# Expert stage of a two-block transformer kernel: order of the score blocks, place of their weight loads, depth of the row gathers

## The chip, the cores and the metric

One Trainium2 chip, one core of it. The metric is the device time of one execution in microseconds (us); less is better. The kernel before takes 3052.63 us, the median of 3 runs (3047.12 to 3056.36).

## The reference, cut to what matters

Two transformer blocks run on 512 tokens of width 1024 in float32. The change lies in the second half of the first block, `peer_ffn`: a mixture of 16384 experts, each of which is one row of a table `u` and one row of a table `v`.

```python
q = (xb @ wq).reshape(T, HEADS, 2, 128)
s = einsum('thpc,hpnc->thpn', q, keys)           # scores against 2 x 128 keys per head
v1, i1 = top_k(s[:, :, 0], 16); v2, i2 = top_k(s[:, :, 1], 16)
sc, pos = top_k(all sums v1 + v2, 16)            # 16 experts per head, 8 heads
idx = i1 * 128 + i2 at pos; gate = softmax(sc)
act = gelu(einsum('td,thkd->thk', xb, u_tab[idx]))
out = einsum('thk,thkd->td', gate * act, v_tab[idx])
```

So every token has 128 of the 16384 experts, and what it needs is gelu(x . u) of each, times its gate, times that expert's row of v, summed.

## The kernel before, in words

**Two ways for two groups of tokens.** Tokens 0 to 383 (`ND`) are computed densely: for all 16384 experts, in 128 blocks of 128, the kernel computes gelu(u_block . x) for every token, multiplies it with a gate table that is zero where the token did not choose the expert, and adds the product with the block's rows of v into six PSUM banks. Tokens 384 to 511 are computed sparsely: their 256 rows (128 of u, 128 of v) are gathered one at a time, row s of all 128 tokens in one indirect DMA from GpSimd (POOL), 512 KB each, into a tile `row`.

**Score blocks.** `s_block(b)` (lines 721 to 739) takes the weights of block b from `uld`, fetches those of block b + 1 if they are not fetched (`u_load`, 713 to 719: one 512 KB DMA on SP's queue into one of three buffers, a rounded copy `uh` on ScalarE (ACT), the rest `ul` on VectorE (DVE), both in three buffers), issues 24 matmuls into one of two PSUM buffers, and evicts them on ACT with Gelu into `st`. Blocks 0 to 13 (`LEAD`) stay on chip in `held`; blocks 14 to 71 (up to `NS`) go to DRAM by a 192 KB DMA on SP (line 737), from one of two buffers, and come back later (`s_again`, 741); blocks 72 to 127 are computed inside the last loop.

**Order in time.** First the queries and the top 16 keys of every head (lines 798 to 819, the matmuls against `keys` on line 812). Then `route(3)`, which gives `idx` of the sparse tokens, `route(0)`, and `gates(0)`, `gates(1)`, `gates(2)`, one for each 128 dense tokens. `gates` (905 to 929) makes the gate table in steps of 8 tokens (`q`): two one-hot tiles `o` on DVE (913), scaling on ACT (916), 16 matmuls into `pg` (920), two evictions into `stg` (921), and for every 32 tokens a 2 MB store of `stg` to `gates_d` on SP (927). In each step `fill(1)` adds one score block and `row_u()` one gathered row of u: it issues the gather of row n + 2 and multiplies row n with the token on DVE (756). In `gates(2)` every second step takes two rows. Rows of this part have three buffers, and there are 56 (`U1`) of them. `fill` ends at block 64 (`NS - HOLD`), which is four steps before the end of `gates(2)`.

**Between the gates and the loop** stand the last seven score blocks, 65 to 71, on lines 1000 to 1017. From line 993 on (`manual_schedule`) each engine keeps the written order; ahead of it the framework orders the instructions of each engine itself. As written, SP's order there is: weights of 66, the first two blocks of v (`v_dma`, 957), weights of 67, store of 65, weights of 68, store of 66, and so on, with the first gate tile (`v_gate(0)`, a 768 KB read of `gates_d`) after the store of 67. On ACT the rounding of block b + 2's weights stands ahead of the Gelu of block b, and the store of block b waits for that Gelu.

**The loop** (1018 to 1044), b = 0 to 127: prepare block b + 1 (`g_mul` and the split of the gated scores, `v_hi` on ACT, `v_lo` on DVE), read scores back or compute a new block, use the gathered rows that are due (`gs`), then 18 matmuls of block b (1043). Up to b = 57 the scores are read back, afterwards a score block is computed in each step. Here rows have eight buffers.

Pools are stacked: those of the stage up to the gates (`hp4`, `tp4q`, `np4`, `tp4`, `rp4`) are closed before those of the loop (`vpool`, `gp`) open in the same memory, and a new tile waits for the readers of what lay there. `keys` (line 768) takes 8 KB of each partition in `hp4` and is read on line 812 alone.

Of the kernel before, what the change touches and what calls it, by code (L numbers as in the profile page):

```python
# [8 lines left out]
F32 = mybir.dt.float32  # L9
# [39 lines left out]
def tile_two_blocks(ctx: ExitStack, tc: tile.TileContext, a: dict, out: bass.AP):  # L49
# [3 lines left out]
    def mk(c, name, bufs, space=None, side=None):  # L53
        kw = dict(space=space) if space is not None else {}
        return c.enter_context(tc.tile_pool(name=name, bufs=bufs, side=side, reuse_waits="tile", **kw))
# [640 lines left out]
    def blin(w, kd, loeng=None):  # L696
        return Lin(wb, w, kd, loeng, bufs=3, rbufs=3)

    with ExitStack() as c1:
# [5 lines left out]
        gw = pk.tile([128, 128], F32, name="gw")  # L705
        act = pk.tile([128, 128], F32, name="act")
        coef = pk.tile([128, 128], F32, name="coef")
        G.memset(acc, 0.0)
        held = {}
        uld = {}  # L710
        rows = {}

        def u_load(b):
            raw = wb.tile([128, KD, 128], F32, tag="wraw", name="uraw", bufs=3)
            nc.sync.dma_start(raw, a["peer_ut"][b])
            uh = wb.tile([128, KD, 128], F32R, tag="whi", name="uh")
            ul = wb.tile([128, KD, 128], F32R, tag="wlo", name="ul")
            split_r(uh, ul, raw, V)
            uld[b] = (uh, ul)

        def s_block(b):
            if b not in uld:
                u_load(b)
            uh, ul = uld.pop(b)
            if b + 1 < 128 and b + 1 not in uld:
                u_load(b + 1)
            ps = pss.tile([128, ND], F32, tag="pss", name="pss")
            n = 0
            for w_, x_ in ((uh, lo), (ul, hi), (uh, hi)):
                for k in range(KD):  # L730
                    PE.matmul(ps, w_[:, k, :], x_[:, k, :ND], start=n == 0, stop=n == 23)  # L731
                    n += 1
            st = pk.tile([128, ND], F32, tag="st" if b < LEAD or b >= NS else "sp", name="st",
                         bufs=LEAD + 2 if b < LEAD or b >= NS else 2)
            S.activation(st, ps, AF.Gelu)  # L735
            if LEAD <= b < NS:
                nc.sync.dma_start(st_d[b - LEAD], st)
            else:
                held[b] = st
# [5 lines left out]
        def gather_dma(s, pool):  # L745
            if s >= 256:
                return
            tab, i = (a["peer_u"], s) if s < 128 else (a["peer_v"], s - 128)
            r = rows[s] = pool.tile([128, D], F32, tag="row", name="row", bufs=8 if s >= U1 else 3)
            G.indirect_dma_start(out=r, out_offset=None, in_=tab,  # L750
                                 in_offset=bass.IndirectOffsetOnAxis(ap=idx[:, i:i + 1], axis=0))

# [10 lines left out]
        with ExitStack() as c2:  # L763
# [1 line left out]
            pps = mk(c2, "pps4", 2, PSUM)  # L765
            ppt = mk(c2, "ppt4", 2, PSUM)
            ppg = mk(c2, "ppg4", 2, PSUM)
            keys = hp_.tile([128, 16, 128], F32, name="keys")
            nc.sync.dma_start(keys, a["keys"])
            io = hp_.tile([128, 128], F32, name="io")  # L770
            G.iota(io, pattern=[[1, 128]], base=0, channel_multiplier=0, allow_small_or_imprecise_dtypes=True)
            vals = hp_.tile([128, 4, 8, 2, 16], F32, name="vals")
# [10 lines left out]
            with ExitStack() as c3:  # L783
                tp = mk(c3, "tp4q", 2)
                np_ = mk(c3, "np4", 3)
                lin = blin(a["wq"], KD)
                for f in range(2):
                    lin.load(f)

                def normed(k):  # L790
                    h = np_.tile([128, T], F32, tag="h", name="h")
                    V.scalar_tensor_tensor(h, xt[:, k, :], vv("norm2_w", k), rb2, op0=ALU.mult, op1=ALU.mult)
                    split_r(hi[:, k, :], lo[:, k, :], h, G)
                    pt = ppt.tile([128, 512], F32, tag="pt", name="pt")
                    PE.transpose(pt[:, :128], h[:, ND:], ident)
                    S.activation(htok[:, k * 128:(k + 1) * 128], pt[:, :128], AF.Copy)

                first_ps = [pps.tile([128, 512], F32, tag="ps", name="ps") for n in range(2)]
                lin.mm_rows([(first_ps[f], f) for f in range(2)], hu, lu)
                for f in range(16):  # L800
                    if f < 2:
                        ps = first_ps[f]
                    else:
                        ps = pps.tile([128, 512], F32, tag="ps", name="ps")
                        lin.mm(ps, f, hu, lu)
                    if f + 2 < 16:
                        lin.load(f + 2)
                    q = tp.tile([128, T], F32, tag="q", name="q")
                    V.tensor_mul(q, ps, rb2)
                    ps = ppt.tile([128, 512], F32, tag="pt", name="ps")  # L810
                    for t in range(4):
                        PE.matmul(ps[:, t * 128:(t + 1) * 128], q[:, t * 128:(t + 1) * 128], keys[:, f, :],
                                  start=True, stop=True)
                    s_ = tp.tile([128, 4, 128], F32, tag="s", name="s", bufs=2)
                    S.activation(s_.rearrange("p t n -> p (t n)"), ps, AF.Copy)
                    for t in range(4):
                        top16(vals[:, t, f // 2, f % 2], ids[:, t, f // 2, f % 2], s_[:, t, :])
                    if f < KD:
                        normed(f)
# [70 lines left out]
            def fill(n):  # L890
                for _ in range(n):
                    if done_[0] < NS - HOLD:
                        s_block(done_[0])
                        done_[0] += 1

            def row_u():

                n = done_[1]
                if n < U1:
                    if n + 2 < U1:  # L900
                        gather_dma(n + 2, rp)
                    gather(n)
                    done_[1] += 1

            def gates(t, tr, other):

                for hf in range(128 // TS):
                    stg = tp.tile([128, 128, TS], F32, tag="stg", name="stg", bufs=2)
                    for q in range(TS // 8):
                        t0 = hf * TS + q * 8  # L910
                        oo = [tp.tile([128, 8, 128], F32, tag=f"o{n}", name=f"o{n}") for n in range(2)]
                        for n in (1, 0):
                            V.tensor_tensor(oo[n], io[:, None, :].to_broadcast([128, 8, 128]),  # L913
                                            tr[:, n, t0:t0 + 8, None].to_broadcast([128, 8, 128]), op=ALU.is_equal)
                        for i in range(8):
                            S.activation(oo[0][:, i, :], oo[0][:, i, :], AF.Copy, scale=tr[:, 2, t0 + i:t0 + i + 1])
                        for e in (0, 4):
                            pg = ppg.tile([128, 4, 128], F32, tag="pg", name="pg")
                            for i in range(4):
                                PE.matmul(pg[:, i, :], oo[1][:, e + i, :], oo[0][:, e + i, :], start=True, stop=True)  # L920
                            S.activation(stg[:, :, q * 8 + e:q * 8 + e + 4], pg.rearrange("p t i -> p i t"), AF.Copy)
                        fill(1)
                        row_u()
                        if t == NT_ - 1 and q % 2:
                            row_u()
                        next(other, None)
                    nc.sync.dma_start(gates_d[t * (128 // TS) + hf], stg)
                for _ in other:
                    pass
# [3 lines left out]
            for n, _ in enumerate(route(NT_, trs)):  # L933
                if n % 2:
                    fill(1)
            for s in range(2):
                gather_dma(s, rp)
            for n, _ in enumerate(route(0, trs)):
                fill(1)
# [9 lines left out]
        with ExitStack() as c2:  # L949
# [46 lines left out]
            def gs(b):  # L996
                return U1 + (256 - U1) * sum(cost[:b]) // sum(cost)


            for b in range(NS - HOLD, NS - HOLD + 2):  # L1000
                if b not in uld:
                    u_load(b)
            for b in range(2):
                v_dma(b, False)
            for b in range(NS - HOLD, NS - 2):
                u_load(b + 2)
                s_block(b)
                if b == NS - HOLD + 2:
                    v_gate(0)
            g_mul(0)  # L1010
            g_split(0)
            v_hi(0)
            v_lo(0)
            for s in range(gs(0), gs(1)):
                gather_dma(s, gp)
            for b in range(NS - 2, NS):
                s_block(b)
            for b in range(128):
                n = b + 1
                if b + 2 < 128:  # L1020
# [452 lines left out]
```

## Time and profile before

| | |
|---|---|
| median of 3 runs | 3052.63 us (3047.12 to 3056.36) |
| the profiled execution, its time | 3042.29 us |
| its span in the trace | 3040.5 us |
| TensorE (PE) busy in the span | 95% |
| DVE, ACT, POOL busy | 62%, 39%, 30% |
| granted TensorE clock, mean | 0.977 of 2.4 GHz |

Times of rows are us from the start of the span. PE is TensorE's matmuls, PEld its weight loads; SPq and POOLq are the queues from which DMAs are issued. Idle time stands in brackets ahead of an instruction, with what ended it. Matmuls are pipelined, so their durations overlap; a score block's 24 matmuls are best read by the distance from one block to the next.

### The profile page before, as it was taken

Reading aid. Unit: us, or ns where it says so; the run is one execution under the profiler, and the core shown is the slowest. Engines: PE = TensorE matmul, PEld = TensorE weight load, DVE = VectorE, ACT = ScalarE, POOL = GpSimd, SP = SyncE. Lnnn points to the kernel's source line nnn. Section 1 sums busy time; section 2 is a strip of 40 time slices with the busy share of each in tenths; the row PEclk is TensorE's granted clock in tenths of the full one; section 3 lists DMA queues with packets and bytes.
Section 4 is the critical chain, followed back from the end, with each engine's and each line's share of the span. In section 5 each row is a group of like instructions: output and inputs, shape, how many; then the busy total and the mean of one; then the engine's idle time right before and its main releaser. Section 6 shows DMA issues by size and latency. Waiting matters only on the chain.

```text
span 3040.5 us, 45240 instructions
## 1 busy us (share of the span) xinstructions
PE 2877.7 (95%) x17733; PEld 2402.8 (79%) x17733; DVE 1896.8 (62%) x3317; ACT 1198.8 (39%) x2073; POOL 924.9 (30%) x584
## 2 busy tenths in 40 slices
PE   8897898999989799999999999999999999999998
PEld 6676776799989677799999977888876666788886
DVE  7567638899987377777777786332258744643311
ACT  6344334237867233333333334332234343433322
POOL 1011135211321111133444324444431233244443
PEclk9899989999999899999999999999999999999999
DMA  3240123257876699999899962333321112323332
GB/s 115 63 129 27 41 77 122 70 164 257 315 271 241 239 303 318 311 327 306 307 315 332 313 218 63 97 97 95 99 93 49 56 56 66 101 91 97 97 96 78
DMA packets 201286, 494.92 MB, mean 163 GB/s; under 512 B 17328, under 2 KB 95152, under 8 KB 199152
## 3 DMA queue, kind: packets, MB, share of 16 engines
q1 hardware_dynamic: 164208, 357.78, 36.0%
q0 software_dynamic: 36864, 134.23, 12.7%
q8 instruction: 140, 2.29, 0.3%
q14 instruction: 74, 0.61, 0.1%
HBM read 446.60 MB, written 45.22 MB: 162 GB/s over the span
## 4 chain that ended last, share of the span: by engine, by line
PE 59%; DVE 21%; issue 7%; ACT 4%; DMA 4%; POOL 2%; SPq 0%; ACTq 0%; DVEq 0%; POOLq 0%
PE ps L141 33%; PE pss L731 8%; PE pv L1043 8%; DVE vl L978 2%; DVE row L756 2%; ACT vh L972 2%; DVE o L913 2%; PE ps L318 2%; DVE ul L71 2%; DMA gate<-gates_d 2%; DMA uraw<-peer_ut 1%; PE po L1287 1%; DVE st L983 1%; PE pg L920 1%; PE ps L1263 1%
## 5 line engine op out<-in xcount | busy, mean ns | idle before, releaser
L71 POOL TENSOR_TENSOR wlo<-wraw,whi 128x1024 fp32r<-128x1024 f32 (+4 forms) x232 | 503.6, 2174 | 775.9 <-ACT whi L70 773.7
L70 ACT ACTIVATE whi<-wraw 128x1024 fp32r<-128x1024 f32 (+4 forms) x320 | 261.7, 823 | 692.2 <-PE ps L141 428.6
L750 POOL DMA_INDIRECT row<-peer_u,idx x128 | 158.1, 1235 | 618.2 <-DVE row L756 427.6
L141 PE MATMUL ps<-lo,whi 128*128 128x512 f32 x1112 | 303.4, 402 | 2.3 <-DVE pad L218 1.4
L141 PE MATMUL ps<-hi,whi 128*128 128x512 f32 x1112 | 295.1, 395 | 0.0
L141 PE MATMUL ps<-hi,wlo 128*128 128x512 f32 x1112 | 293.9, 395 | 1.1 <-POOL wlo L71 0.7
L141 PEld LDWEIGHTS ps<-lo,whi 128*128 128x128 f32 x1112 | 208.1, 190 | 55.6 <-issue 11.0
L1043 PE MATMUL pv<-vl,gh 128*128 128x512 f32 x768 | 243.1, 398 | 6.8 <-DVE vl L978 4.3
L141 PEld LDWEIGHTS ps<-hi,wlo 128*128 128x128 f32 x1112 | 208.0, 189 | 51.5 <-issue 6.3
L750 POOL DMA_INDIRECT row<-peer_v,idx x128 | 168.6, 1317 | 256.7 <-DVE acc L761 219.3
L141 PEld LDWEIGHTS ps<-hi,whi 128*128 128x128 f32 x1112 | 207.6, 188 | 47.1 <-issue 5.2
L1043 PE MATMUL pv<-vh,gl 128*128 128x512 f32 x768 | 239.0, 392 | 1.9 <-ACT vh L972 1.9
L1043 PE MATMUL pv<-vh,gh 128*128 128x512 f32 x768 | 239.6, 393 | 0.0
L70 ACT ACTIVATE gh<-st 128x384 fp32r<-128x384 f32 x128 | 67.2, 525 | 414.2 <-DVE st L983 224.2
L731 PE MATMUL pss<-lo,uh 128*128 128x384 f32 x1024 | 210.5, 347 | 17.6 <-ACT st L735 17.4
L731 PE MATMUL pss<-hi,ul 128*128 128x384 f32 x1024 | 203.4, 339 | 4.0 <-DVE ul L71 4.0
L731 PEld LDWEIGHTS pss<-lo,uh 128*128 128x128 f32 x1024 | 183.2, 192 | 23.6 <-ACT st L735 19.2
L731 PE MATMUL pss<-hi,uh 128*128 128x384 f32 x1024 | 199.5, 336 | 0.0
L978 DVE TENSOR_TENSOR vl<-vraw,vh 128x1024 fp32r<-128x1024 f32 x128 | 161.4, 1261 | 50.1 <-ACT vh L972 49.7
L71 DVE TENSOR_TENSOR ul<-uraw,uh 128x1024 fp32r<-128x1024 f32 x128 | 156.2, 1220 | 53.3 <-ACT uh L70 53.3
L731 PEld LDWEIGHTS pss<-hi,ul 128*128 128x128 f32 x1024 | 182.6, 191 | 4.7 <-DVE ul L71 4.7
L1043 PEld LDWEIGHTS pv<-vl,gh 128*128 128x128 f32 x768 | 141.4, 189 | 52.0 <-DVE vl L978 23.6
(445 smaller groups left out, 5236.6 us busy)
## 6 DMA issues: line engine op xcount, KB each, us to landing
uraw<-peer_ut SPq DMA_DIRECT2D x128, 512.0 KB, 6.2
vraw<-peer_v SPq DMA_DIRECT2D x128, 512.0 KB, 5.5
wraw<-ffn_w_in SPq DMA_DIRECT2D x88, 512.0 KB, 3.5
gates_d<-stg SPq DMA_DIRECT2D x12, 2048.0 KB, 9.2
gate<-gates_d SPq DMA_DIRECT2D x32, 768.0 KB, 8.1
wraw<-w_in SPq DMA_DIRECT2D x40, 512.0 KB, 3.5
wraw<-ffn_w_out SPq DMA_DIRECT2D x32, 512.0 KB, 3.5
st_d<-st SPq DMA_DIRECT2D x58, 192.0 KB, 4.2
```

Of the source, the lines that this page charges most:

```text
L70: S.activation(hi, src, AF.Copy)
L71: eng.tensor_sub(lo, src, hi)
L141: PE.matmul(ps, w_[:, k, :m], x_[:, k0 + k, :], start=n == 0, stop=n == last)
L318: PE.matmul(ps[j:j + 64], w_[j:j + 64], x_[j:j + 64], start=start, stop=stop, tile_position=(j, j))
L731: PE.matmul(ps, w_[:, k, :], x_[:, k, :ND], start=n == 0, stop=n == 23)
L750: G.indirect_dma_start(out=r, out_offset=None, in_=tab, in_offset=bass.IndirectOffsetOnAxis(ap=idx[:, i:i + 1], axis=0))
L756: V.scalar_tensor_tensor(r, r, 1.0, htok, op0=ALU.mult, op1=ALU.mult, accum_out=act[:, s:s + 1])
L913: V.tensor_tensor(oo[n], io[:, None, :].to_broadcast([128, 8, 128]), tr[:, n, t0:t0 + 8, None].to_broadcast([128, 8, 128]), op=ALU.is_equal)
L920: PE.matmul(pg[:, i, :], oo[1][:, e + i, :], oo[0][:, e + i, :], start=True, stop=True)
L972: S.activation(vh, vld[b], AF.Copy)
L978: V.tensor_sub(vl, raw, vh)
L1043: PE.matmul(pv[t * 2 + e], l_[:, ts_], r_[:, e * 512:(e + 1) * 512], start=b == 0 and q == 0, stop=b == 127 and q == 2)
```

## The change

1. The score blocks are computed in another order, `seq`: blocks 14 to 71 first, then 0 to 13, then 72 to 127. So the seven blocks between the gates and the loop are 7 to 13, which stay on chip and are not stored. (The prediction counts blocks by their place in the order; places 65 to 71 are those between the gates and the loop, in both kernels.)
2. In the last four steps of `gates(2)` the weights of places 66 and 67 are fetched and rounded.
3. The part between the gates and the loop is written anew: one block of v (not two) is fetched after place 65, the gate tile and the second block of v after place 67; POOL copies one column of the scores of place 68 into a tile `fence`, and its gathers stand behind that copy; the preparation of loop step 0 stands after place 69.
4. Rows of u up to 56 have five buffers in place of three, and row n + 4 in place of n + 2 is gathered ahead; four rows in place of two are gathered before `route(0)`.
5. `keys` moves from the pool `hp4` to the pool `np4`, which is closed before the gates begin.

```diff
+        fence = pk.tile([128, 1], F32, name="fence")
+        seq = list(range(LEAD, NS)) + list(range(LEAD)) + list(range(NS, 128))
+        place = {b: n for n, b in enumerate(seq)}
...
-            if b + 1 < 128 and b + 1 not in uld:
-                u_load(b + 1)
+            n = place[b] + 1
+            if n < 128 and seq[n] not in uld:
+                u_load(seq[n])
...
-            r = rows[s] = pool.tile([128, D], F32, tag="row", name="row", bufs=8 if s >= U1 else 3)
+            r = rows[s] = pool.tile([128, D], F32, tag="row", name="row", bufs=8 if s >= U1 else 5)
...
-            keys = hp_.tile([128, 16, 128], F32, name="keys")
-            nc.sync.dma_start(keys, a["keys"])
...
+                keys = np_.tile([128, 16, 128], F32, name="keys", bufs=1)
+                nc.sync.dma_start(keys, a["keys"])
...
-                        s_block(done_[0])
+                        s_block(seq[done_[0]])
...
-                    if n + 2 < U1:
-                        gather_dma(n + 2, rp)
+                    if n + 4 < U1:
+                        gather_dma(n + 4, rp)
...
+                        if t == NT_ - 1 and hf == 128 // TS - 1 and q >= 2:
+                            for n in seq[done_[0]:done_[0] + q]:
+                                if n not in uld:
+                                    u_load(n)
...
-            for s in range(2):
+            for s in range(4):
                 gather_dma(s, rp)
...
-            for b in range(NS - HOLD, NS - HOLD + 2):
-                if b not in uld:
-                    u_load(b)
-            for b in range(2):
-                v_dma(b, False)
-            for b in range(NS - HOLD, NS - 2):
-                u_load(b + 2)
-                s_block(b)
-                if b == NS - HOLD + 2:
+            for n in range(NS - HOLD, NS):
+                if n < NS - 2 and seq[n + 2] not in uld:
+                    u_load(seq[n + 2])
+                s_block(seq[n])
+                if n == NS - HOLD:
+                    v_dma(0, False)
+                if n == NS - HOLD + 2:
                     v_gate(0)
-            g_mul(0)
-            g_split(0)
-            v_hi(0)
-            v_lo(0)
-            for s in range(gs(0), gs(1)):
-                gather_dma(s, gp)
-            for b in range(NS - 2, NS):
-                s_block(b)
+                    v_dma(1, False)
+                if n == NS - 4:
+                    G.tensor_copy(fence, held[seq[n]][:, 0:1])
+                    for s in range(gs(0), gs(1)):
+                        gather_dma(s, gp)
+                if n == NS - 3:
+                    g_mul(0)
+                    g_split(0)
+                    v_hi(0)
+                    v_lo(0)
```

## Rows read from the trace of the kernel before

**Rows 1.** Busy time in stretches of the expert stage (columns in the first row).

```profile
core 0: us, PE busy (x) PEld busy (x) DVE busy (x) ACT busy (x) POOL busy (x), PEclk, DMA share, GB/s
700.00:860.00 160.00, 158.73 (x1055) 158.45 (x1056) 157.85 (x247) 134.23 (x337) 31.62 (x23) 0.98 0.76 267
890.00:945.00 55.00, 46.68 (x292) 46.00 (x291) 42.09 (x54) 33.21 (x85) 19.35 (x14) 0.94 0.89 321
993.00:1043.00 50.00, 32.56 (x154) 31.18 (x154) 8.55 (x9) 9.62 (x14) 7.33 (x7) 0.83 0.66 233
```

**Rows 2.** The chain that ended last, 960 to 1046: start us, us, what.

```profile
960.18 4.17 PE pss L731 x24
964.35 1.78 PE pg L920 x16
...
995.54 10.74 DMA uraw<-peer_ut
...
1040.81 3.45 DMA uraw<-peer_ut
```

**Rows 3.** What PE waited for, 993 to 1045.

```profile
PE pss L731 <- ACT st L735: 17.4, 4, 9.5
```

**Rows 4.** What ACT waited for, 993 to 1045: us in total, times, longest.

```profile
ACT uh L70 <- DMA uraw<-peer_ut: 40.1, 6, 12.6
```

**Rows 5.** Order of time on SP's queue: the last store of the gate table.

```profile
993.75 0.32 SPq L927 DMA_DIRECT2D gates_d<-stg  x1
```

**Rows 6.** What PE waited for, 840 to 992.

```profile
PE pg L920 <- ACT stg L921: 9.0, 2, 4.5
PE pg L920 <- ACT o L916: 3.8, 1, 3.8
```

**Rows 7.** What DVE waited for, 840 to 992.

```profile
DVE row L756 <- DMA row<-peer_u,idx: 20.2, 10, 6.4
```

**Rows 8.** Stretches with a lower granted clock (columns as in rows 1).

```profile
883.00:887.00 4.00, 3.70 (x18) 3.70 (x19) 4.00 (x6) 1.97 (x4) 3.35 (x2) 0.57 0.82 258
...
900.00:907.00 7.00, 5.79 (x23) 5.80 (x24) 7.00 (x8) 6.25 (x18) 1.85 (x2) 0.52 1.02 390
...
1002.00:1013.00 11.00, 5.21 (x16) 5.21 (x17) 1.23 (x1) 1.43 (x2) 6.39 (x6) 0.53 1.01 390
...
1050.50:1054.00 3.50, 3.50 (x10) 2.73 (x9) 2.65 (x3) 1.38 (x2) 0.00 (x0) 0.51 0.99 340
```

**Rows 9.** Order of time on PE at the loop's start.

```profile
1042.41 0.63 PE L1043 MATMUL pv<-vh,gl 128*128 128x512 f32 x2
...
1048.62 0.73 PE L1043 MATMUL pv<-vh,gl 128*128 128x512 f32 x2 [1.93 <-ACT vh L972]
1049.88 0.50 PE L1043 MATMUL pv<-vl,gh 128*128 128x512 f32 x1 [0.52 <-DVE vl L978]
```

**Rows 10.** Issue to landing of gathered rows, 700 to 990.

```profile
DMA to landing us min/median/max: 4.2/7.6/13.0
```

**Rows 11.** Evictions of stored score blocks, 660 to 697: min/median/max ns, first to last.

```profile
L735 ACT ACTIVATE st<-pss x8: 491/493/495, 663.2 to 692.3; 128x384 f32<-128x384 f32 x8
```

**Rows 12.** Order of time on POOL, 984 to 1012: first and last of eight gathers.

```profile
988.51 0.99 POOL L750 DMA_INDIRECT row<-peer_u,idx  x1 [47.67 <-ACT o L916]
...
1009.73 0.94 POOL L750 DMA_INDIRECT row<-peer_u,idx  x1 [0.30 <-issue]
```

**Rows 13.** Order of time on DVE: the loop's first gathered row.

```profile
1053.06 1.22 DVE L756 SCALAR_TENSOR_TENSOR row<-row,htok 128x1024 f32<-128x1024 f32 x1
```

**Rows 14.** The keys: their DMA on SP, and their first reader on PE.

```profile
482.99 0.42 SPq L769 DMA_DIRECT2D keys<-keys  x1
...
495.07 1.06 PE L812 MATMUL ps<-keys,q 128*128 128x128 f32 x8
```

**Rows 15.** Issue to landing of the 2 MB stores of the gate table.

```profile
DMA to landing us min/median/max: 6.5/9.2/13.3
```

**Rows 16.** Issue to landing of the score blocks' weights, 700 to 990.

```profile
DMA to landing us min/median/max: 3.4/5.6/11.2
```

## The prediction

> **What bounds the kernel now.** I read the page first: TensorE (PE) is busy nearly throughout and leads the chain that ended last, so what the change can win is time in which PE stands still or runs at the lower of its clocks. Then the table of stretches over the expert stage, to see where that is. From 700 to 860 PE is busy 158.73 of 160 us: the gates are bound by PE, at one step of 4.17 + 1.78 = 5.95 us (a score block and 16 gate matmuls) [rows 1, 2]. From 890 to 945 it is busy 46.68 of 55, and between the gates and the loop, 993 to 1043, 32.56 of 50, with a mean clock of 0.83 [rows 1]. The reader is to see in the waits what ends these two losses.
>
> *Between gates and loop* PE waits 17.4 us in four pieces for ACT's Gelu, which frees the PSUM buffer [rows 3]. The Gelu isn't slow: ACT itself waits 40.1 us, six times, for weights [rows 4]. The chain shows the circle: the load of place 67 goes out at 995.54, behind the 2 MB gate store of 993.75, and takes 10.74 us [rows 2, 5]; only then come rounding, the Gelu of place 65, its store on SP's queue, and behind that store the next load. Six loads, the last at 1040.81, follow each other so, one in flight at a time. A block of 4.17 us of work is thus paid with a whole landing.
>
> *In the last gates* PE waits 9.0 + 3.8 = 12.8 us in three pieces for the one-hot tiles [rows 6]. DVE makes these late because it stands 20.2 us, ten times, for gathered rows [rows 7]; its own order is fixed, so a row that has not landed stops the gate work behind it. After each stop the granted clock is at its lower level of 1.2 GHz for a while: 0.57 from 883 to 887, 0.52 from 900 to 907 [rows 8].
>
> **The change part by part.** The sum is made against the profiled execution, 3042.29 us (span 3040.5); the median of the three runs, 3052.63, lies 10.3 us (0.34%) above it, and I subtract the gain from the median.
>
> *A. Blocks kept on chip made last, weights fetched beside the gates.* No store stands between the loads on SP, and places 66 and 67 are rounded when the gates end. PE can run places 66 to 71 from the moment place 66 starts now, about 994 (just behind the gate store's issue): 6 x 4.17 = 25.0 us, so the loop could begin at 1019.0, against 1042.41 [rows 2, 5, 9]. What stays is the load of place 68. It goes out behind the 2 MB store and one block of v. Bounds: at the 390 GB/s of the crowded stretch 1002 to 1013 [rows 8], 2048 + 512 + 512 KB (3.15 MB) take 8.1 us, landing at 1001.8, which is before PE has done 66 and 67 (994 + 8.3 = 1002.3): only rounding shows, about 1 us. Scaled from the load of place 67 today, which landed at 1006.28 behind 3.67 MB (12.5 us from the store's issue), it is 10.7 us, landing at 1004.5, and 1.5 us later PE may start: a gap of 3.7. I take 3, nearer to the second, because it is the same queue at the same moment, and 1 us for a lower clock after it. Loop start 994 + 25.0 + 4 = 1023.0, a gain of **19.4**. Bounds 22.4 and 12: the poor end is a further wait for places 70 and 71, priced below as a rival. The rounding of place 67, one pass on ACT and one on DVE, lands in the last four gate steps, in which `fill` adds no score block; free, or 2 us if not.
>
> *B. The weights of place 72* go out today at 1040.81 and hold up ACT as the loop begins [rows 2]. PE then waits 1.93 + 0.52 us, and the clock is at 0.51 from 1050.5 to 1054, half of 3.5 us lost, 1.7 [rows 8, 9]. They will be fetched with the rest, some 10 us ahead: **4.2**. Bounds 0 (the loop stumbles over something else) and 4.6.
>
> *C. Four rows in flight.* At stake: 12.8 us of waits plus 0.43 x 4 + 0.48 x 7 = 5.1 us of low clock [rows 6, 8], 17.9 in all, and a third low stretch as a margin of 1.6. A row lands in 7.6 us in the median and 13.0 at most [rows 10]; two ahead at two rows in a 5.95 us step cover about 6 us, four cover 12. So the median row no longer stops DVE and the worst still does. Bandwidth is there: 321 GB/s in this stretch [rows 1] against 390. I take **13**. Bounds 19.5 and a loss of 5 (PE waits 12.8 us in three, so one more such stop is 4.3, with its clock some 5): outside the hand-ordered part the framework orders DVE's work anew and may place rows worse.
>
> *D. Fourteen stores earlier.* Places 0 to 13 now go to DRAM, SP carrying 14 stores that it didn't carry there. Eight stored blocks were evicted from 663.2 to 692.3, 4.16 us apart [rows 11], the pace of PE's own work: stores cost nothing there now. 0; if that cover is gone, 14 issues on SP's queue show, 0.32 us each as the store of [rows 5], some 5 us.
>
> *E. The fence, and gathers behind it.* The copy of one column is tiny, but eight gathers stand behind it on POOL, and POOL waits for the Gelu of place 68, which PE ends at 1002.3 + 3 + 4.2 = 1009.5 and which on ACT stands behind the rounding of place 70: about 1011, against 988.51 to 1009.73 today [rows 12]. They are first read at 1053.06, 10.7 us after the loop begins [rows 9, 13]. With a loop start of 1023 that is 1033.7; issued at 1011 and 13.0 us in flight the first lands by 1025. 0, with some 9 us to spare.
>
> Against this stands a rule of the Trainium skill, page "DMA: Bandwidth & Descriptors", section "Rules for kernel authors": issue a DMA early and wait for it late. By it the 22 us of delay would be a loss wherever the landing is waited for; [rows 12, 13] show landings that lie unread for over 40 us, so here the trace does not bear it out; by the rule the sum would be 3019 to 3023 (rival 3), by the rows it is 3016.
>
> *F. The keys* are issued at 482.99 and first read at 495.07 [rows 14]. In the new place they wait for other readers, but stand on SP behind the same store. 0, bounds 0 and 3 lost.
>
> Sum: 19.4 + 4.2 + 13 = 36.6. On the profiled execution 3005.7, on the median **3016.0 us**, 1.2% faster.
>
> **The rivals.**
> 1. *The rows stay late.* If rows are held up by bandwidth and not by depth (the stretch 900 to 907 moved 390 GB/s [rows 8]), C gives 2: 3027. Against it: 321 in the mean.
> 2. *A new wait on SP's queue.* The first gate tile reads what the 2 MB store of 993.75 writes and so must wait for its landing, 9.2 us in the median, 13.3 at most [rows 5, 15]; behind it stand the second block of v and the loads of 70 and 71. Median: SP free at 1003, 1.8 MB more at 390 GB/s, place 70 landed at 1008, needed at about 1014: hidden. With 13.3 and a landing of 11.2 [rows 16] it comes at 1019: 5 to 7 us lost with the clock, A is 12: 3023.
> 3. *Late rows in the loop*: gathers that issue only as the loop begins (1023) land up to 13.0 us later [rows 10], at 1036 to 1037 against 1033.7, 3 us, and as much again for the queue of eight: 3019 to 3023. It needs a fence 10 us later than I reckon. So the rule of the Trainium skill named above would show.
> 4. *Slower: weights starved by rows.* Four rows in flight put 1 MB more beside each load of weights, at 390 GB/s 2.7 us. With three buffers loads run two steps ahead, 11.9 us; they land in 5.6, at most 11.2 [rows 16]. Beyond 11.9 each step costs half the excess, over the 44 blocks of the gates. To lose A, B and 9 us more it takes 0.75 us a block, a landing of 13.4 as the rule: 3062 and more. 5.6 + 2.7 = 8.3 speaks against.
> 5. *The change doesn't do what it says.* The framework may place the two early loads behind the gate store, and the rows no better: then A shrinks to a few us, C to 0, 3046.
>
> **How the numbers follow.** Forecast (A, B and most of C) 0.56; rival 1 0.20; rival 2 0.09; rival 3 0.05; rival 4 0.04; rival 5 0.06. About 0.3% (9 us) is what a measurement of this kernel can tell from no change. Forecast and rivals 1 to 3 are faster by more: 0.90; rival 5 is the same, 0.06; rival 4 slower, 0.04. The forecast's own range is 3006 (all three upper bounds) to 3024; rivals 1 and 2 together reach 3034. With two us for the spread of the runs: 3004 to 3036.
>
> **What would show it right or wrong.** A: in the changed trace the loads of places 68 to 72 go out without a store between, PE waits once, 1 to 4 us, from place 66 to the loop, and that stretch is 26 to 31 us long. B: the loop's first two steps are 4.1 to 4.5 us apart. C: DVE's wait for rows under 7 us and no stop of PE over 3 in the gates. E: no DVE wait for rows in the loop. Wrong if PE still stands over 10 us before the loop, or if the gates' DVE waits stay near 20.

## The result and the profile after

The changed kernel takes **3007.09 us** (median of 4 runs, 3002.81 to 3008.72), against 3053.02 us for the kernel before (median of 4 runs): a ratio on record of 0.9857 with a 95% interval of 0.9842 to 0.9873, so 1.4% faster (the two medians alone give 0.985). The forecast was 3016.0 us in a range of 3004 to 3036, with a chance of 0.90 for faster. It holds; the gain is larger than forecast, 45.9 us between the medians against 36.6.

The profiled execution of the changed kernel took 3002.81 us (span 3001.0), 4.3 us below the median of its runs, as that of before (span 3040.5) lay 10.3 us below its own. The two spans differ by 39.5 us. Cut at the matmuls that begin and end each stage, they differ here:

| stage, us in the span | before | after | gain | forecast |
|---|---|---|---|---|
| start to the first gate matmul | 701.3 | 697.5 | 3.8 | F: 0 |
| the three gate stages | 291.8 | 275.6 | 16.2 | C: 13 |
| last gate matmul to the loop | 49.3 | 31.7 | 17.6 | A: 19.4 |
| loop steps 0 and 1 | 12.8 | 8.2 | 4.7 | B: 4.2 |
| loop steps 2 to 57 | 246.7 | 246.6 | 0.1 | 0 |
| loop steps 58 to 127 | 524.1 | 521.1 | 3.0 | 0 |
| the rest, which the change doesn't touch | 1214.5 | 1220.5 | -6.0 | 0 |

**The gates.** The same stretches as [rows 1] and [rows 8] and the gap between gates and loop, and in the last row the one low-clock stretch that is left between 701 and 1060 (columns in the first row):

```profile
core 0: us, PE busy (x) PEld busy (x) DVE busy (x) ACT busy (x) POOL busy (x), PEclk, DMA share, GB/s
700.00:860.00 160.00, 160.00 (x1075) 159.69 (x1075) 158.57 (x251) 135.12 (x337) 32.88 (x22) 1.00 0.76 269
882.00:912.00 30.00, 27.78 (x183) 27.46 (x182) 29.10 (x36) 22.16 (x59) 18.96 (x11) 1.00 1.00 370
...
973.70:1005.40 31.70, 27.23 (x147) 26.83 (x146) 8.87 (x9) 9.35 (x16) 10.06 (x9) 0.95 0.88 309
987.20:990.60 3.40, 3.40 (x13) 3.40 (x12) 1.25 (x2) 0.52 (x2) 0.00 (x0) 0.50 1.02 403
```

PE is busy for the whole of the first stretch, and from 882 to 912 the clock stays at 1.00, where it had dropped to 0.57 and 0.52 [rows 8]. The low stretches went with the stops. The waits of PE, then of DVE, from 835 to 972 (us in total, times, longest):

```profile
PE pg L925 <- ACT o L921: 2.2, 1, 2.2
...
DVE row L761 <- DMA row<-peer_u,idx: 2.8, 3, 1.0
```

Against [rows 7], 20.2 us in ten waits became 2.8 in three, and PE's 12.8 us of [rows 6] became 2.2. A row isn't any quicker: issue to landing is now 8.8 us in the median and 12.9 at most, against 7.6 and 13.0 [rows 10]. It is asked for earlier.

**Between gates and loop.** The chain that ended last (start us, us, what):

```profile
973.74 0.33 SPq L936
...
974.59 10.30 DMA uraw<-peer_ut
...
984.91 1.06 ACT uh L70
985.97 0.39 ACT st L740
...
986.40 18.53 PE pss L736 x96
1004.93 4.09 PE pv L1053 x18
```

The circle of [rows 2] (load, rounding, Gelu, store, next load) is broken: one load lies on the chain, that of place 68, and behind it PE runs four blocks without a gap. PE's and ACT's waits from 972 to 1007:

```profile
PE pss L736 <- ACT st L740: 4.5, 1, 4.5
...
ACT uh L70 <- DMA uraw<-peer_ut: 14.6, 2, 10.8
```

Of PE's 17.4 us in four pieces [rows 3] one of 4.5 is left. The order of time, of SP's queue, then the rounding of place 70 on ACT, POOL's gathers and DVE's first row in the loop:

```profile
973.74 0.33 SPq L936 DMA_DIRECT2D gates_d<-stg  x1
974.12 0.42 SPq L968 DMA_DIRECT2D vraw<-peer_v  x1
974.59 2.21 SPq L719 DMA_DIRECT2D uraw<-peer_ut  x2
981.06 0.38 SPq L975 DMA_DIRECT2D gate<-gates_d  x1
981.49 2.07 SPq L968 DMA_DIRECT2D vraw<-peer_v  x1
983.62 5.33 SPq L719 DMA_DIRECT2D uraw<-peer_ut  x3
...
991.55 1.06 ACT L70 ACTIVATE uh<-uraw 128x1024 fp32r<-128x1024 f32 x1 [3.83 <-DMA uraw<-peer_ut]
...
993.05 0.86 POOL L1020 COPY fence<-st 128x1 f32<-128x1 f32 x1 [80.77 <-ACT st L740]
994.07 1.96 POOL L755 DMA_INDIRECT row<-peer_u,idx  x1 [0.16 <-DMA vraw<-peer_v]
...
1004.62 0.94 POOL L755 DMA_INDIRECT row<-peer_u,idx  x1 [0.30 <-issue]
...
1011.75 1.22 DVE L761 SCALAR_TENSOR_TENSOR row<-row,htok 128x1024 f32<-128x1024 f32 x1
```

Two loads go out right behind the 2 MB store and one block of v (places 68 and 69); the gate tile's read waits for the store to land, 7.3 us, and three more loads (70 to 72) go out behind it, with no store among them. The eight gathers stand behind the fence.

**The rest.** From the loop's end on, the two kernels are the same, and yet the stage differs by 6.0 us in these two executions. It isn't of the change: it also differs between two kernels described below (both fetch three loads early, the first without the fence, the second with it), and goes with the granted clock. From the loop's end to the end of the span, one after the other:

```profile
1780.70:2995.70 1215.00, 1177.19 (x5388) 925.45 (x5386) 539.58 (x848) 412.33 (x651) 461.03 (x208) 0.99 0.27 83
```

```profile
1776.70:2999.20 1222.50, 1184.81 (x5389) 931.09 (x5387) 539.83 (x848) 411.97 (x651) 460.94 (x208) 0.98 0.27 83
```

The other engines were busy equally long; PE took 7.6 us more at a clock of 0.98 instead of 0.99. In all the profiles this stage is 1214.5 to 1222.7 us long, and the changed kernel measured twice more had 1214.6 and 1217.8. A difference of a few us between two spans therefore proves nothing; the experiments are read by their stages, and by their ratios over several runs.

### The profile page after: what moved, and what is told of

Same layout as the page of the kernel before. It is cut to its first block, busy times and chain, and to the rows that moved or that the text cites. A ratio compares the mean times of both kernels' runs of the same rounds, so it can differ in the third digit from the quotient of the medians.

```text
span 3001.0 us, 45236 instructions
## 1 busy us (share of the span) xinstructions
PE 2869.5 (96%) x17733; PEld 2397.2 (80%) x17733; DVE 1895.7 (63%) x3317; ACT 1198.9 (40%) x2073; POOL 932.8 (31%) x585
## 3 DMA queue, kind: packets, MB, share of 16 engines
q0 software_dynamic: 36864, 134.23, 12.8%
## 4 chain that ended last, share of the span: by engine, by line
PE 64%; DVE 19%; issue 5%; ACT 4%; DMA 3%; POOL 2%; ACTq 0%; SPq 0%; DVEq 0%; POOLq 0%
PE ps L141 33%; PE pss L736 13%; PE pv L1053 8%; DVE vl L987 2%; ACT vh L981 2%; DVE row L761 2%; PE ps L318 2%; PE pg L925 2%; DMA gate<-gates_d 2%; DVE o L918 1%; PE po L1297 1%; DVE ul L71 1%; POOL wlo L71 1%; DVE st L992 1%; PE ps L1273 1%
## 5 line engine op out<-in xcount | busy, mean ns | idle before, releaser
L755 POOL DMA_INDIRECT row<-peer_u,idx x128 | 164.7, 1287 | 489.5 <-DVE row L761 354.3
L736 PEld LDWEIGHTS pss<-hi,uh 128*128 128x128 f32 x1024 | 180.3, 189 | 0.0
```

The costliest lines, as they stand in the source:

```text
L755: G.indirect_dma_start(out=r, out_offset=None, in_=tab, in_offset=bass.IndirectOffsetOnAxis(ap=idx[:, i:i + 1], axis=0))
```

## The experiments

The theory to be tried: C is a matter of how far ahead the rows are asked for, A of the stores between the loads and of what shares the queues with them, and the two add. The rivals were those of the prediction, and one more that arose from the trace: that the fence, costed at nothing, does something.

**One part at a time: the order alone.** The kernel before, with the new order of the blocks and nothing else:

```diff
+        seq = list(range(LEAD, NS)) + list(range(LEAD)) + list(range(NS, 128))
...
-            for b in range(NS - HOLD, NS - 2):
-                u_load(b + 2)
-                s_block(b)
-                if b == NS - HOLD + 2:
+            for n in range(NS - HOLD, NS - 2):
+                u_load(seq[n + 2])
+                s_block(seq[n])
+                if n == NS - HOLD + 2:
```

> Only the order of the score blocks is changed; the part between the gates and the loop, the rows (two ahead) and the keys stay as in the kernel before. Theory (the stores between the weight loads chained them): with no store on SP between loads, the small waits vanish (3.05 + 0.92 + 4.0 us and their low clock) and the loop's first two steps are near 4.1 us, but the load of place 67 still stands behind the gate store and two blocks of v, so the first wait of about 9.5 us stays. From place 66 to the loop 38 to 40 us instead of 48.4; 11 to 15 us faster than before in all, gates unchanged. Rival (landing times, not the stores, set the pace): 46 to 49 us from place 66 to the loop, no gain over 4 us.

Measured: 3028.7 us, a ratio of 0.9936 (0.9916 to 0.9955). The stretch from the last gate matmul to the loop fell from 49.3 to 38.7 us and the first two loop steps from 12.8 to 8.2; the gates stayed at 291.5. So the order alone gives 10.6 of A's 17.6 us and all of B. What is left, PE's waits from 991 to 1031:

```profile
PE pss L735 <- ACT st L739: 9.8, 2, 9.6
```

**One part at a time: the rows alone.** The kernel before, with four rows in flight (and the keys at their new place):

```diff
-            ... bufs=8 if s >= U1 else 3)
+            ... bufs=8 if s >= U1 else 5)
...
-                    if n + 2 < U1:
-                        gather_dma(n + 2, rp)
+                    if n + 4 < U1:
+                        gather_dma(n + 4, rp)
...
-            for s in range(2):
+            for s in range(4):
```

> Only the depth of the row gathers (four ahead, five buffers) and, to make room, the place of the keys are changed against the kernel before. Theory (depth alone cures the late rows): DVE's wait for rows in the gates falls from 20.2 us to about 3, PE's three stops of 12.8 us vanish, the gates take 276 us instead of 292, and the part between gates and loop stays at 48 to 50 us; 14 to 18 us faster than before. Rival (the new order of blocks made the gates faster): the gates stay at 288 us or more and the gain is under 5 us.

Measured: 3028.49 us, 0.9932 (0.9917 to 0.9948). The gates take 276.1 us, 15.7 less, and the stretch behind them 48.4, against 49.3 before. DVE's waits for rows from 840 to 985:

```profile
DVE row L756 <- DMA row<-peer_u,idx: 3.8, 4, 1.8
```

**And the reverse: the change without the deeper rows.** The same three places set back in the changed kernel.

> The changed kernel with the rows as before: two ahead, three buffers. Theory (parts add): the gates are back at about 292 us with 20 us of DVE waits for rows, the part from place 66 to the loop stays at about 31 us; 14 to 18 us slower than the changed kernel, so 28 to 32 us faster than before. Rival (the new order made the gates faster): within 5 us of the changed kernel.

Measured: 3024.25 us, 0.9914 (0.9899 to 0.993). Gates 293.2 us; between gates and loop 31.6 as in the changed kernel. DVE's waits from 840 to 991:

```profile
DVE row L761 <- DMA row<-peer_u,idx: 20.7, 9, 6.8
```

C is thus worth 15.7 us added to the kernel before and 17.6 taken from the changed one. The parts don't lean on each other: 10.6 + 4.6 and 15.7 from the two single runs make 30.9 of the 38.5 us; most of the other 7.6 lie in the new arrangement between gates and loop. In their stages the three runs came out close to the theories; in the total time they didn't: against the median of the kernel before, the order alone is 19.5 us faster (11 to 15 expected), the rows alone 19.7 (14 to 18), the change without the deeper rows 23.9 (28 to 32).

**Three rows in flight.** The changed kernel with four buffers, n + 3 and `range(3)`.

> The changed kernel with three rows ahead and four buffers in place of four and five. Theory (a row in flight covers 3 us of a landing of 7.6 us in the median, so three cover the median and four the tail): DVE waits for rows 4 to 9 us, the gates take 277 to 282 us, 1 to 6 us slower than the changed kernel. Rival 1 (three are enough): within 1 us in the gates. Rival 2 (depth has to cover the worst landing of 13 us): 12 us of waits or more, gates at 286 us or more.

Measured: 3011.33 us, 0.9885 (0.9866 to 0.9904); gates 284.0 us. DVE's waits from 840 to 980, then PE's from 840 to 975:

```profile
DVE row L761 <- DMA row<-peer_u,idx: 9.8, 8, 2.2
...
PE pg L925 <- ACT o L921: 5.7, 1, 5.7
PE pg L925 <- ACT stg L926: 2.2, 2, 2.0
```

The gates lie between the theory's 277 to 282 us and the second rival's 286 and more, and the waits between 9 and 12 us, so neither was met; the first rival is refuted. Depths 2, 3 and 4 give 20.7, 9.8 and 2.8 us of waits and gates of 293.2, 284.0 and 275.6 us. The loss falls with the distance, while the traffic is the same, so it was the distance, not the bandwidth.

**The fence away.** The changed kernel without one line:

```diff
-                    G.tensor_copy(fence, held[seq[n]][:, 0:1])
```

> The changed kernel without the copy into the fence, so that the loop's first gathers may issue when their buffers come free. Theory 1 (the fence protects the weight loads): some of the eight gathers move beside the gate store and the loads of places 68 to 71, place 68 starts 2 to 4 us later and the loop begins 2 to 5 us later. Theory 2 (the fence is worth nothing): the stretch from place 66 to the loop is 31.3 us within 1, and the time that of the changed kernel within 3 us. Theory 3 (issuing late costs, as the rule has it): faster than the changed kernel by 2 us or more.

Measured: 3012.07 us, 0.9878 (0.986 to 0.9896), and between gates and loop 41.0 us in place of 31.7. Order of time of SP's queue, then POOL, then ACT:

```profile
978.50 0.33 SPq L936 DMA_DIRECT2D gates_d<-stg  x1
...
987.91 5.67 SPq L719 DMA_DIRECT2D uraw<-peer_ut  x3
...
986.77 0.94 POOL L755 DMA_INDIRECT row<-peer_u,idx  x1 [71.16 <-DMA vraw<-peer_v]
...
995.59 0.94 POOL L755 DMA_INDIRECT row<-peer_u,idx  x1 [0.30 <-issue]
...
1006.33 1.06 ACT L70 ACTIVATE uh<-uraw 128x1024 fp32r<-128x1024 f32 x1 [13.98 <-DMA uraw<-peer_ut]
```

PE's waits from 970 to 1017, 4.5 us in the changed kernel:

```profile
PE pss L736 <- ACT st L740: 10.0, 2, 5.8
```

The gathers go out from 8.3 us behind the store on, the load of place 70 follows 9.4 us behind the store, and this load is rounded 18.4 us after its issue (987.91 to 1006.33). In the changed kernel the same load goes out about as late behind its store (983.62 against 973.74) and is rounded 7.9 us later, at 991.55. What the queues moved (packets, MB, share), from 987.9 to 1006.3 without the fence:

```profile
DMA packets 3381, 7.25 MB, mean 394 GB/s; under 512 B 212, under 2 KB 1839, under 8 KB 3380
...
q1 hardware_dynamic: 2475, 3.92, 57.9%
q0 software_dynamic: 905, 3.31, 45.8%
```

and with it, from 983.6 to 991.6:

```profile
DMA packets 2157, 3.00 MB, mean 375 GB/s; under 512 B 80, under 2 KB 1616, under 8 KB 2157
...
q1 hardware_dynamic: 2157, 3.00, 106.0%
```

The total is about the same, 394 and 375 GB/s. Without the fence the gathers' queue (q0) takes 3.31 of 7.25 MB, and the loads on SP's queue (q1) get 213 GB/s in place of 375. A load that PE needs next shares about evenly with eight that DVE needs some 20 us later. The first theory was right in kind and wrong in place and size: place 68 comes no later (its rounding starts 10.9 us behind the store, 11.2 with the fence), it is place 70, and the loss is 9.3 us, not 2 to 5. 5.5 of it are waits of PE, the other 3.8 time at the lower clock (0.50 from 1007 to 1012). The second and third theories are refuted in this stretch. The total time alone would not tell: the ratio of 0.9878 lies above the changed kernel's 0.9857 to 0.9874, and the intervals overlap. This run's gates, too, took 278.4 us in place of 275.6, and whether the copy has to do with that stays open.

The page "DMA: Bandwidth & Descriptors" of the Trainium skill, section "Queues, rings and completion order", says that each DMA engine takes turns between the queues for which it has work. The split of 54 to 46 in bytes is near what even turns would give; the turns themselves no run shows.

**The loads ahead of the store.** The changed kernel, with the DMAs (not the rounding) of places 68 to 70 issued ahead of the last gate store:

```diff
+                        if t == NT_ - 1 and hf == 128 // TS - 1 and q == 3:
+                            u_raw(seq[done_[0] + 3])
+                            u_raw(seq[done_[0] + 4])
+                            u_raw(seq[done_[0] + 5])
```

> The changed kernel with the DMAs of the weights of places 68, 69 and 70 (not their rounding) put ahead of the last gate store, in the last gate step. Theory (what is left between gates and loop is one landing behind the 2 MB store): PE's wait of 4.5 us at place 68 and the low clock after it go, the stretch from place 66 to the loop is 25 to 28 us instead of 31.3, and the kernel is 4 to 6 us faster than the changed one. Rival (the wait moves on): places 71 or the first gate tile become late and the stretch stays at 30 to 32 us; or the three loads delay the last gate steps by 2 us or more, and nothing is won.

Measured: 2997.58 us, 0.9835 (0.9819 to 0.9851), beside 3003.07 for the changed kernel on the same chip. Between gates and loop it takes 25.3 us, which is PE's own work, with no wait and no low clock (columns as in the first fence):

```profile
980.70:1006.00 25.30, 25.30 (x145) 24.95 (x144) 9.32 (x11) 9.28 (x14) 8.34 (x9) 1.00 0.97 359
```

**The same without the fence,** to see what the fence guards.

> The version with the three loads of places 68 to 70 ahead of the last gate store, without the fence copy; the gathers then issue some 7 to 8 us earlier. Theory 1 (the fence guards one load, that of place 70, which is now out before the gathers): the stretch between gates and loop stays at 25.3 us, within 1, and the time within 2 us of the version with the fence. Theory 2 (it guards every load that goes out beside the gathers, so now those of places 71 and 72): PE or the first loop steps wait for one of these, the stretch and the first two loop steps together grow from 33.5 to 38 to 43 us, and the time by 4 to 9 us.

Measured: 2998.71 us, 0.9855 (0.9839 to 0.9871), against 3000.93 us with the fence on the same chip. The eight gathers go out from 986.52 on, and the stretch is again 25.3 us (columns as in the first fence):

```profile
971.00:996.30 25.30, 25.30 (x157) 24.82 (x156) 6.74 (x7) 12.47 (x29) 7.65 (x8) 1.00 0.78 275
```

In order of time, on POOL and ACT:

```profile
986.52 0.94 POOL L762 DMA_INDIRECT row<-peer_u,idx  x1 [69.51 <-DMA gates_d<-stg]
...
995.71 1.06 ACT L70 ACTIVATE uh<-uraw 128x1024 fp32r<-128x1024 f32 x1 [4.35 <-DMA uraw<-peer_ut]
```

The first theory holds: once the load of place 70 is out, the fence is worth nothing. ACT does wait 4.35 us for the load of place 71, which goes out at 987.11 beside the gathers; PE doesn't notice.

**The fence in the old arrangement.** The order alone, as in the first run, with the same copy ahead of its gathers.

> The new block order in the old arrangement between gates and loop (both blocks of v first, weights two ahead), with the fence put ahead of the eight gathers. It completes a square: old arrangement without fence 38.7 us from the last gate matmul to the loop, new without 41.0, new with 31.7. Theory (it is the gathers' traffic beside the weights of places 68 to 72 that delays them, in either arrangement): the gathers issue some 10 us later than 986 to 1008, the stretch falls to 31 to 34 us, PE's waits in it from 9.8 us to under 6, and the time lies 4 to 8 us below the new order alone, a ratio to before of about 0.9915. Rival (the fence only makes good what the new arrangement itself spoiled, by putting v behind the weights): 38 to 39 us as without it, ratio 0.9936.

Measured: 3029.31 us, 0.9957 (0.9943 to 0.9971), against 3028.7 us for the order alone on another chip. The stretch is 35.8 us, 2.9 less than without a fence; PE's waits from 991 to 1028:

```profile
PE pss L736 <- ACT st L740: 8.1, 1, 8.1
```

Neither expectation was met: the stretch lies between the 31 to 34 of the one and the 38 to 39 of the other, and in the whole time nothing of it can be seen. What is left is the wait for place 67, whose load goes out behind the store and two blocks of v and is rounded at 1003.77, ahead of the fence and of every gather; place 70 is rounded 5.5 us after its issue, 13.1 without the fence. Fence and arrangement belong together, as the four stretches show:

| gates' end to loop, us | without fence | with fence |
|---|---|---|
| old arrangement (two blocks of v ahead of the loads) | 38.7 | 35.8 |
| new arrangement (one block of v ahead) | 41.0 | 31.7 |

Only the fence differs within a row of the table; the new arrangement also has four rows in flight and the keys moved. With the fence the rows make no difference to the stretch (31.6 us with two in flight); without it that wasn't tried. The new arrangement without a fence is 2.3 us worse than the old one. Counted from the last gate matmul, its eight gathers go out 8.9 to 17.8 us behind it, six of the old one's 9.7 to 16.8 us, so in both they meet the load of place 70; why the new one loses more is not shown.

**The four lines that fetch places 66 and 67 in the gates, away.**

```diff
-                        if t == NT_ - 1 and hf == 128 // TS - 1 and q >= 2:
-                            for n in seq[done_[0]:done_[0] + q]:
-                                if n not in uld:
-                                    u_load(n)
```

> The changed kernel without the four lines that fetch the weights of places 66 and 67 in the last gate steps. Theory (the loads of 66 and 67 come early because no load of v and no store stands ahead of them in the written order, so the framework moves them up by itself): the stretch from place 66 to the loop stays at 31 to 33 us and the time within 3 us of the changed kernel. Rival (the four lines do it): place 67 starts only after a landing behind the gate store, as before the change, and the stretch is 38 to 41 us, 7 to 10 us slower than the changed kernel.

Measured: 3005.78 us, 0.9862 (0.9845 to 0.9878), beside 3003.07 for the changed kernel; the stretch is 31.7 us as with them. Here too only the loads of places 68 and 69 follow the store; the framework puts the other two ahead of it by itself. The lines are worth nothing.

**The changed kernel again,** twice, as the measure for its neighbours, and the early loads a second time.

> The changed kernel again, as the reference for the kernels beside it. Expected: 1.3 to 1.6% faster than before, the gates at 276 us, 31 us from place 66 to the loop.

> The changed kernel unaltered, as the measure for the runs beside it: ratio to before 0.9857 to 0.9864, as it had; between gates and loop 31 to 33 us.

> The version with three loads ahead of the gate store once more, beside the changed kernel on one chip. If what it takes away (4.5 us of PE waits and 6 us at the lower clock, 6.4 us of the stretch) reaches the end: 5 to 7 us below the changed kernel, ratio to before 0.984. If the first difference was the spread between executions: within 2 us of it.

Measured: the changed kernel 3003.07 us, 0.9864 (0.9846 to 0.9883), and 3002.74 us, 0.9874 (0.9859 to 0.9888), with 32.2 and 32.3 us between gates and loop; the early loads 3000.93 us, 0.9862 (0.9846 to 0.9878), with 25.3 us. The stretch is 6.8 and 7.0 us shorter, but the whole only 5.5 us the first time and 1.8 the second, which by the last expectation is no more than spread, and both times the intervals overlap; the second ratio of the changed kernel also lies above the 0.9857 to 0.9864 expected. The profiles show where part of it goes. The gates take 1.9 and 0.7 us longer, loop steps 2 to 57 take 248.1 and 251.0 us in place of 246.8, and from the first gate matmul to the loop's end 3.5 and 1.9 us are left; the untouched rest was 6.6 and 4.7 us longer in these executions. In the second pair DVE waited twice as long for gate tiles in loop steps 2 to 57, with the early loads and then without:

```profile
DVE st L1003 <- DMA gate<-gates_d: 8.4, 6, 2.5
DVE st L992 <- DMA gate<-gates_d: 4.2, 4, 1.7
```

Whether the early loads cause this is not shown. That early loads gain between gates and loop is shown; that the whole program gains the same is not.

## Why the prediction was right

**A, forecast 19.4, measured 17.6.** The mechanism is the one described: no store between the loads, places 66 and 67 ready, one wait of PE for place 68. Its test was missed by little, 31.3 us from the start of place 66 (973.45) to the loop against 26 to 31, a wait of 4.5 against 1 to 4, since both parts of what stays were put too low: the load of place 68 landed 11.2 us after the store's issue (973.74 to 984.91); the two bounds had been 8.1 and 10.7, and the wait was 4.5 us in place of 3. The lower clock cost 1.9 us in place of 1: four blocks took 18.53 us, at 4.17 each they take 16.7, and the stretch 987.2 to 990.6 ran at 0.50, the lower of the two levels (1.2 GHz). The order alone brought 10.6 us; 7.0 came with the new arrangement.

**B, forecast 4.2, measured 4.7** (4.6 with the order alone). The two steps take 4.08 us each.

**C, forecast 13, measured 16.2** (15.7 and 17.6 in the single runs). This is the term that was mis-sized most. The step that failed is "the median row no longer stops DVE and the worst still does": the worst landing is still 12.9 us, and yet the longest wait of DVE is 1.0 us. Of the sum at stake, 17.9 + 1.6, 16.2 us came. What was wrong is the cover, counted as a steady 12 us for four rows with two rows in each step; only every second step takes two, and in the changed trace the last twenty rows of the gates, issued from 855 on, have 7.5 to 15.9 us between issue and use. The slowest of them landed in 12.8 us and had 13.6 (issued at 885.24, read at 898.85, in the rows below), the longest wait was for one that had 9.0 (873.94 and 882.90):

```profile
873.94 1.97 POOL L755 DMA_INDIRECT row<-peer_u,idx  x1 [0.31 <-issue]
885.24 1.98 POOL L755 DMA_INDIRECT row<-peer_u,idx  x1 [0.30 <-issue]
...
882.90 1.23 DVE L761 SCALAR_TENSOR_TENSOR row<-row,htok 128x1024 f32<-128x1024 f32 x1 [1.00 <-DMA row<-peer_u,idx]
...
898.85 1.22 DVE L761 SCALAR_TENSOR_TENSOR row<-row,htok 128x1024 f32<-128x1024 f32 x1
```

That the slowest rows met long distances may be luck; no run tries it.

**D and F, forecast 0.** The 14 stores cost next to nothing: from 600 to 700 ACT waits 2.8 us, twice, for one of them to free its buffer, and PE 0.5 us for ACT. From the start to the first gate matmul the changed kernel was 3.8 us quicker; 2.2 of it lie before the keys are first used, a stretch that took 491.2 to 498.2 us in the various runs. The other 1.6 seem to belong to the change: from the first use of the keys to the first gate matmul it is 206.1 to 206.4 us in the three kernels with the keys at their old place and 203.2 to 205.5 in all others. Why is not shown.

**E, forecast 0, was right for the cost and wrong for the role.** No row comes late in the loop (the first is read at 1011.75, without a wait), 17.7 us after its gather went out. But the fence was taken for a step without effect, and it holds 9.3 us of A. The step that failed is to have asked only who waits for the gathers, not what they take from others. That A came near its forecast is luck in this respect: its sum has no term for what the fence keeps away. The rule of the Trainium skill weighed there (page "DMA: Bandwidth & Descriptors", section "Rules for kernel authors": issue early, wait late) points the other way, and for these gathers the runs speak against it: issued early, ahead of the load of place 70, they cost 9.3 us, and issued late nothing. With that load out first, issuing them early cost nothing either (25.3 us both ways).

**The sum.** A, B and C measured make 38.5 us against 36.6, and the spans differ by 39.5; from the first gate matmul to the loop's end it is 41.7. The medians differ by 45.9 us, and by 44.9 and 40.4 in the two repetitions. What the sum doesn't hold are 3.0 us in loop steps 58 to 127, and the differences at the start and in the rest, of both signs. The 3.0 us have no wait behind them, as PE is busy throughout in both kernels there; the order alone and the rows alone don't show them, but the order with the fence does (458.0 us for steps 58 to 113, against 461.0), and so do all kernels made from the changed one, without the fence too. Their cause stays open.

**The rivals.** Rows late by bandwidth (1): refuted by the depths of 2, 3 and 4. A new wait on SP's queue (2): it is there, the gate tile's read holding the queue from 977 to 981.06 and with it the loads of 70 to 72; PE doesn't feel it as long as the loads behind it have the queues for themselves, and without the fence it does. Late rows in the loop (3): no such wait. Weights starved by rows (4): the loads of the score blocks land in 6.0 us in the median and 10.9 at most, against 5.6 and 11.2 [rows 16]. The change doesn't do what it says (5): for four lines true, the framework having done the same already; for the gain not.

## What to carry to other kernels

Where an engine works through a fixed order, ask for gathered data well ahead of the median landing; here the third row in flight was worth 9.2 us and the fourth 8.4, with a median landing of 8.8 us in the end, and a fifth wasn't tried. A prefetch that nobody needs yet isn't free when it goes out beside a load that the bound engine needs next: hold it back behind something that comes after that load, or issue that load first, which makes the holding back unnecessary. And a gain of a few us is to be read from its own stage and those right behind it, which may give part of it back, as the rest of a long program can move by more from one execution to the next.

## What the runs showed of the hardware

A load of 512 KB landed in 7.8 us when only its own queue had work and in 18.3 us when eight gathers on POOL's queue went out at the same time, at nearly equal total rates (375 and 394 GB/s), the two queues moving 3.92 and 3.31 MB. In the untouched second part of the program the time of PE varied by 7.6 us between executions, at granted clocks of 0.99 and 0.98.
